# First feed-forward block of a decoder layer: ada products spread over other stages, finished tiles gated in two stages, first channel blocks in written order

## The chip, the core and the metric

One core of a Trainium2 chip runs the whole layer as one program. TensorE (PE; its weight loads are listed as PEld) multiplies, VectorE (DVE), ScalarE (ACT) and GpSimd (POOL) do the elementwise work, and SyncE's queue (SP) issues the DMA transfers in program order. The metric is the time of one execution in microseconds, as the median of the runs.

## What is computed

A decoder layer on x of 256 positions and 1024 channels, float32: a half-step SwiGLU block, a mixer of attention and mLSTM heads, and a second SwiGLU block. Each is preceded by an RMS norm whose scale and shift, and followed by a gate, that come from a vector c.

```python
mod = (c @ w_ada + b_ada).reshape(B, 9, D_MODEL)       # 72 columns of 128 values
sh1, sc1, g1, sh2, sc2, g2, sh3, sc3, g3 = ...
h = modulate(rmsnorm(x, ffn1_norm), sh1, sc1)          # h * (1 + sc) + sh
x = x + 0.5 * (1 + g1) * swiglu(h, w_gate, w_up, w_down)   # D_FF = 2816 = 22 tiles of 128
h = modulate(rmsnorm(x, mix_norm), sh2, sc2)
x = x + (1 + g2) * hybrid_mixer(h, ...)
h = modulate(rmsnorm(x, ffn2_norm), sh3, sc3)
x = x + 0.5 * (1 + g3) * swiglu(h, ...)                # second block, then a final norm
```

## The kernel before

**Products in three passes.** Channels lie on the partitions. Every float32 weight chunk (`raw`, 128 x 2048, 1 MB) is split into a rounded part `whi` (ACT) and the rest `wlo` (DVE), in two pieces of 1024 columns (`split_piece`, lines 199 to 211); activations are split likewise into `hh` and `hl`. `mm3` (line 232) adds whi x hh, wlo x hh and whi x hl. There are 4 buffers for `raw` and 5 each for `whi` and `wlo`. `weights()` (line 219) hands out the next chunk, asks for the load of the chunk three ahead and the split of the next one.

**Ada products.** `ada(col)` (line 247) loads 512 KB of w_ada into one of 3 buffers (one SP transfer) and has DVE multiply it by c and sum it along the row: one column of `mod`. Sixteen columns (scale and shift of the first norm) are made on the spot, two for each of the eight channel blocks. The other 56 are jobs in a list, and `side(...)` (line 551) pops one job for each of its arguments; eight jobs make one of scale, shift or gate.

**First feed-forward block** (`ffn`, k = 0, lines 402 to 494). Each of the 22 tiles of the hidden width needs a gate and an up half, which share one PSUM bank. The work is staged so that the eight channel blocks can be used as they come:
- first blocks: for channel blocks d = 0 to 3, eight tiles (0 to 7) are accumulated in all eight banks. d = 0 is done in plain float32 by `first`, d = 1 to 3 by `outer`, each on one chunk of 48 matmuls. Ahead of block d the program makes the two ada products, the scale, shift and `norm_h` (line 323: DVE `ht`, ACT `hh`, DVE `hl`) and the split of block d + 1. After d = 3 the banks are copied to `half`;
- tiles 8 to 15 on channel blocks 0 to 3 (`inner`, four chunks), then on blocks 4 to 7 (`outer`, four chunks), again in eight banks (`ps`);
- tiles 0 to 7 on channel blocks 4 to 7 (`inner` with d0 = 4, four chunks, lines 481 to 492; below the second inner stage). Each gets a fresh bank, is added to `half`, and is gated by `finish`. Between them the tiles 8 to 15 in `ps` are gated too (`late`), which frees their banks;
- tiles 16 to 21 one by one, then the down projection (11 chunks, 176 pairs of matmuls).

`finish` (line 375) is ACT silu into `sl`, DVE product into `gm`, then ACT and DVE split that into `gh`, `gl`. `sl` and `gm` have two buffers each, given out in program order.

**Banks.** `BANKS` has 2 of tag b, 2 of m and 4 of a. `ring` (line 395) names the tag of each tile of eight: b, m, a, a, b, m, a, a.

**Order.** Instructions sent through `Ordered` with `on` set keep their program order on their engine. All others are put in order by the framework's planner on a simulated timeline when the kernel is built. DMA issues always keep their order. `ordered(d == 0)` (line 451) keeps the written order for the first channel block only.

**After the block.** `residual` (line 358) adds a finished output block to x, and makes that block's part of the next norm's input (`pre_h`) and its square (`add_sq`); `pre_shift` adds the shift's two columns. The first projection of the mixer (`px`, lines 563 to 572) and the mixer follow. Late in the mixer a chain of small steps ends in `rows` (`m_factors`, `spread`), which `m_spread` (PE) needs amid the output projection (`wout`, line 1000).

Of the kernel before, what the change touches and what calls it, by code (L numbers as in the profile page):

```python
# [17 lines left out]
P = 128  # L18
# [42 lines left out]
def layer(ctx: ExitStack, tc: tile.TileContext, i, out: bass.AP):  # L61
# [4 lines left out]
    def ordered(on):  # L66
        for e in (act, dve, pool, pe):
            e.on = on
# [15 lines left out]
    def bank(tag):  # L84
        return psp.tile([P, 512], F32, tag=tag, name=nm("ps" + tag), bufs=BANKS[tag])
# [7 lines left out]
    def const(shape, dt, name):  # L93
        return cst.tile(shape, dt, tag=name, name=name)
# [41 lines left out]
    for k in range(2):  # L136
        pe.matmul(pc[k], ones_r, c_hl[:, k * 512:(k + 1) * 512], start=True, stop=True)
    warm(2)
    act.activation(c_bc[:, 0:512], pc[0], AF.Copy)
    dve.tensor_tensor(sq[:, 0:4], x_sb[:, 0:4], x_sb[:, 0:4], ALU.mult)  # L140
    dve.tensor_tensor(sq[:, 0:2], sq[:, 0:2], sq[:, 2:4], ALU.add)
    act.activation(sq[:, 4:8], x_sb[:, 4:8], AF.Square)
    act.activation(c_bc[:, 512:1024], pc[1], AF.Copy)
    dve.tensor_tensor(sq[:, 4:6], sq[:, 4:6], sq[:, 6:8], ALU.add)

    ident = const([P, P], F32, "ident")
# [19 lines left out]
        pool.affine_select(out=oh32, in_=oh32, compare_op=ALU.not_equal, fill=1.0, base=base,  # L166
                           pattern=[[1, NH], [0, P]], channel_multiplier=-1)
    ohr = const([36, NH, P], F32R, "ohr")
    dve.tensor_copy(ohr, oh32)


    SP = 1024
# [64 lines left out]


    mod = const([P, 72], F32, "mod")
    b1 = const([P, 72], F32, "b1")  # L240
    dve.tensor_scalar(b1, sm[:, 0:72], 1.0, None, ALU.add)
    gs = [const([P, ND], F32, f"gs{k}") for k in range(3)]
    sh = [const([P, ND], F32, f"sh{k}") for k in range(3)]
    gt = [const([P, ND], F32, f"gt{k}") for k in range(3)]
# [36 lines left out]
    def scale_jobs(k):  # L281
        return ada_jobs(24 * k + 8, lambda: scale_fin(k))
# [59 lines left out]
    def hilo(hi, lo, src):  # L342
        act.activation(hi, src, AF.Copy)
        dve.tensor_tensor(lo, src, as32(hi), ALU.subtract)
# [13 lines left out]
    def residual(d, ps, g, k):  # L358
        dve.scalar_tensor_tensor(x_sb[:, d], ps, g[:, d:d + 1], x_sb[:, d], ALU.mult, ALU.add)
        if k is None:  # L360
            s = add_sq(d, pool)
            pool.tensor_scalar(fin_u[0][:, d], x_sb[:, d], sm[:, C_NF + d:C_NF + d + 1], None, ALU.mult)
            return s
        if d == ND - 1:
            s = add_sq(d, pool)
            pre_h(k, d)
        else:
            pre_h(k, d)
            s = add_sq(d, pool)
        return s  # L370
# [4 lines left out]
    def finish(gh, gl, ft, g, u):  # L375
        s = t256("sl")
        act.activation(s, g, AF.Silu)
        m = t256("gm")
        dve.tensor_tensor(m, s, u, ALU.mult)
        hilo(gh[:, ft], gl[:, ft], m)  # L380
# [16 lines left out]
    def ffn(k, nxt):  # L397
        nfa = 3
        with tc.tile_pool(name=f"g{k}", bufs=1) as gp:
            g2 = gp.tile([P, NF, 2, T], F32R, name=f"g2{k}")  # L400
            gh, gl = g2[:, :, 0], g2[:, :, 1]
            if k == 0:
# [45 lines left out]
                parts.append([raws[0][:, k * SP:(k + 1) * SP] for k in range(2)])  # L448
                used[0] += 1
                for d in range(4):  # L450
                    ordered(d == 0)
                    if d < 3:
                        adas(d + 1)
                        load_to(d + 1)
                        fins(d + 1)
                        split_to(d + 1)
                        w = parts[d]
                        used[0] += d > 0
                    else:
                        w = weights()  # L460
                    if d == 0:
                        first(raws[0], ps, h0)
                    else:
                        outer(w, ps, d, False, keep if d == 3 else None)
                    if d == 1:
                        hilo(hh[:, 0, 0:T], hl[:, 0, 0:T], h0)
                ps = [bank(t) for t in ring]
                for j in range(4):
                    w = weights()
# [3 lines left out]
                        inner(w, f2, ps[2 * j + f2], 0, False)  # L473
                for d in range(4, 8):
                    w = weights()
                    if d > 5:
                        side(1, 0)
                    outer(w, ps, d, d == 7)
                late = [lambda ft=ft, pb=pb: finish(gh, gl, 8 + ft, pb[:, 0:T], pb[:, T:2 * T])
                        for ft, pb in enumerate(ps)]  # L480
                for j in range(4):
                    late.pop(0)()
                    late.pop(0)()
                    w = weights()
                    side(1, 1)
                    for f2 in range(2):
                        ft = 2 * j + f2
                        pb = bank(ring[ft])
                        inner(w, f2, pb, 4, True)
                        o = half[:, ft]  # L490
                        dve.tensor_tensor(o, o, pb, ALU.add)
                        finish(gh, gl, ft, o[:, 0:T], o[:, T:2 * T])
                late = []
                nfa = 16
            else:
                ps = [bank(t) for t in ("b", "b", "a", "a", "a", "a")]
# [9 lines left out]
            for ft in range(nfa, NF):  # L506
                if late:
                    late.pop(0)()
                w = weights()
                if late:  # L510
                    late.pop(0)()
                side(*QF[k])
                if k == 0:
                    pb = bank(ring[ft % 8])
                    for d in range(ND):
                        for g in range(2):
                            mm3(pb[:, g * T:(g + 1) * T], w, (d * 2 + g) * P, hh[:, d, 0:T], hl[:, d, 0:T],
                                start=(d == 0 and g == 0), stop=(d == ND - 1))
                    finish(gh, gl, ft, pb[:, 0:T], pb[:, T:2 * T])
                else:  # L520
                    pb = [bank("maba"[ft % 4 - 3]) for g in range(2)]
                    for g in range(2):
                        for d in range(ND):
                            mm3(pb[g][:, 0:W], w, (g * ND + d) * P, hh[:, d], hl[:, d],
                                start=(d == 0), stop=(d == ND - 1))
                    finish_pre(gh, gl, ft, pb[0], pb[1], r)
# [24 lines left out]
    def side(*on):  # L551

        for o in on:
            if jobs:
                jobs.pop(0)(o)


    jobs += scale_jobs(1) + gate_jobs(0) + shift_jobs(1) + gate_jobs(1) + scale_jobs(2) + shift_jobs(2)
    ffn(0, 1)

    px = [bank("a") for _ in range(4)]
    for c in range(2):
        w = weights()
        side(1)
        for d4 in range(4):
            d = c * 4 + d4
            for h in range(NH):
                mm3(px[h][:, 0:W], w, d4 * 512 + h * P, hh[:, d], hl[:, d], start=(d == 0), stop=(d == 7))  # L570
            if d == 0:
                r = rstd_of([acc, nxt_sq[0]], pre=False)
# [15 lines left out]
def mixer(tc, nc, i, mp, L):  # L588
# [377 lines left out]
    m_scores(3)  # L966
    m_sums(1)
    g = tiles(shifted(zs[:, 0]), shifted(zs[:, 1]))
    side(1)
    next(g)  # L970
    next(g0)
    turn(3)
# [26 lines left out]
    po = [bank(t) for t in ("m", "m", "a", "a")]  # L999
    for c in range(4):  # L1000
        w = weights()
        pe.on = c < 2
        for k2 in range(2):
            k = c * 2 + k2
            for d in range(8):
                mm3(po[d // 2][:, (d % 2) * T:(d % 2 + 1) * T], w, (k2 * 8 + d) * P, *mix(k),
                    start=(c == 0 and k2 == 0 and d % 2 == 0), stop=(c == 3 and k2 == 1))
                if (k, d) == (2, 7):
                    m_spread()
                    for h in range(NH):  # L1010
                        m_out(h)
# [90 lines left out]
```

## Time and profile before

| | |
|---|---|
| median of 3 runs | 534.91 us (534.86 to 535.97) |
| the profiled execution | 537.05 us, of which the span from first to last instruction is 535.2 us |
| PE busy | 517.4 us (97%), 3804 matmuls |
| DVE busy | 423.4 us (79%) |
| ACT busy | 281.0 us (53%) |
[...]
| DMA | 125.73 MB, 235 GB/s over the span |

Busy PE time counts a matmul from start to modelled end, and they overlap; how many matmuls start in a stretch says more. A row of the timeline gives start, duration, engine, operation, and in brackets the idle time of that engine just before and what ended it.

### The profile page before, as it was taken

How to read it: one execution, taken by the hardware profiler on the slowest of the kernel's cores; microseconds unless marked ns; L12 is line 12 of the kernel's file. 1: busy time of each engine (PE TensorE's matmuls, PEld its weight loads, DVE VectorE, ACT ScalarE, POOL GpSimd, SP SyncE). 2: the span in 40 equal slices, each digit the busy share in tenths (PEclk: the TensorE clock that was granted, in tenths of full speed). 3: DMA queues.
4: the chain of work that ended last, by engine and by line, in shares of the span. 5: the costliest groups of instructions: out<-in, count | busy, mean ns of one | idle time of the engine just before them, and what ended most of it. 6: DMA issues, size and time to landing. Idle time of an engine off the chain costs nothing.

```text
span 535.2 us, 9560 instructions
## 1 busy us (share of the span) xinstructions
PE 517.4 (97%) x3804; PEld 485.3 (91%) x3804; DVE 423.4 (79%) x714; ACT 281.0 (53%) x486; POOL 46.9 (9%) x64
## 2 busy tenths in 40 slices
PE   7999999899999999999999989999999999999992
PEld 7899999899988889988987889999999999988881
DVE  7898879999889997898885686989986776655423
ACT  4464436355555544566767554865545455544410
POOL 5000000000001110110000020400000000022220
PEclk9999999899999999999999999999999999999998
DMA  8997977988778998578631024488955455455002
GB/s 311 356 411 298 381 282 294 349 351 325 300 286 329 328 344 303 172 287 319 225 146 59 15 105 141 184 326 293 312 195 186 163 196 193 157 206 188 1 1 78
DMA packets 23951, 125.73 MB, mean 235 GB/s; under 512 B 2657, under 2 KB 2913, under 8 KB 14434
## 3 DMA queue, kind: packets, MB, share of 16 engines
q1 hardware_dynamic: 23618, 124.59, 62.2%
q8 instruction: 30, 0.49, 0.4%
q10 hardware_dynamic: 288, 0.52, 0.3%
q14 instruction: 15, 0.12, 0.1%
HBM read 124.05 MB, written 1.05 MB: 234 GB/s over the span
## 4 chain that ended last, share of the span: by engine, by line
PE 89%; DVE 4%; DMA 3%; issue 2%; ACT 1%; SPq 0%; DVEq 0%; ACTq 0%
PE psa L54 42%; PE psb L54 27%; PE psm L54 21%; DMA ada<-in_ada 2%; DMA x<-in_x 1%; DVE junk L54 1%; DVE wlo L54 1%; ACT whi L54 0%; DVE cn L54 0%; DVE u_out L54 0%; ACT sq L54 0%; DVE nw L54 0%; DVE half L54 0%; ACT zs L54 0%; DVE x L54 0%
## 5 line engine op out<-in xcount | busy, mean ns | idle before, releaser
L54 ACT ACTIVATE whi<-raw 128x1024 fp32r<-128x1024 f32 (+1 forms) x160 | 167.2, 1047 | 137.8 <-PE psa L54 62.4
L54 DVE TENSOR_TENSOR wlo<-raw,whi 128x1024 fp32r<-128x1024 f32 (+1 forms) x160 | 193.3, 1211 | 53.2 <-ACT whi L54 51.8
L54 PE MATMUL psa<-hh,whi 128*128 128x258 f32 (+1 forms) x388 | 110.1, 286 | 0.6 <-DVE gm L54 0.6
L54 PE MATMUL psa<-hh,wlo 128*128 128x258 f32 (+1 forms) x388 | 110.3, 286 | 0.0
L54 PE MATMUL psa<-hl,whi 128*128 128x258 f32 (+1 forms) x388 | 108.8, 285 | 0.0
L54 PE MATMUL psb<-hh,whi 128*128 128x258 f32 (+1 forms) x316 | 91.3, 290 | 2.3 <-ACT hh L54 1.2
L54 DVE SCALAR_TENSOR_TENSOR junk<-ada,c_bc 128x1024 bf16<-128x1024 f32 x72 | 88.1, 1224 | 3.4 <-DMA ada<-in_ada 3.3
L54 PE MATMUL psb<-hh,wlo 128*128 128x258 f32 (+1 forms) x316 | 89.4, 284 | 0.0
L54 PE MATMUL psb<-hl,whi 128*128 128x258 f32 (+1 forms) x316 | 88.9, 283 | 0.0
L54 PEld LDWEIGHTS psa<-hh,whi 128*128 128x128 f32 x388 | 74.4, 192 | 0.8 <-DVE gm L54 0.8
L54 PEld LDWEIGHTS psa<-hh,wlo 128*128 128x128 f32 x388 | 74.4, 192 | 0.1
L54 PEld LDWEIGHTS psa<-hl,whi 128*128 128x128 f32 x388 | 73.9, 192 | 0.0
L54 PEld LDWEIGHTS psb<-hh,whi 128*128 128x128 f32 x316 | 59.8, 189 | 5.3 <-issue 1.4
L54 PEld LDWEIGHTS psb<-hh,wlo 128*128 128x128 f32 x316 | 59.7, 189 | 0.1
L54 PEld LDWEIGHTS psb<-hl,whi 128*128 128x128 f32 x316 | 59.7, 190 | 0.0
L54 PE MATMUL psa<-g,whi 128*128 128x512 f32 x176 | 59.4, 395 | 0.0
L54 PE MATMUL psm<-hh,wlo 128*128 128x256 f32 (+1 forms) x200 | 56.9, 285 | 0.0
L54 PE MATMUL psm<-hh,whi 128*128 128x256 f32 (+1 forms) x200 | 56.8, 284 | 0.0
L54 PE MATMUL psm<-hl,whi 128*128 128x256 f32 (+1 forms) x200 | 56.6, 285 | 0.0
L54 PE MATMUL psa<-g,wlo 128*128 128x256 f32 x176 | 45.5, 281 | 0.0
L54 PEld LDWEIGHTS psa<-g,whi 128*128 128x128 f32 x176 | 32.5, 188 | 7.2
L54 PEld LDWEIGHTS psm<-hh,whi 128*128 128x128 f32 x200 | 38.2, 191 | 0.2
(241 smaller groups left out, 768.3 us busy)
## 6 DMA issues: line engine op xcount, KB each, us to landing
ada<-in_ada SPq DMA_DIRECT2D x72, 512.0 KB, 6.0
raw<-in_dn SPq DMA_DIRECT2D x22, 1024.0 KB, 4.8
raw<-in_guB SPq DMA_DIRECT2D x19, 1024.0 KB, 4.8
raw<-in_gu SPq DMA_DIRECT2D x18, 1024.0 KB, 7.1
raw<-in_gu SPq DMA_DIRECT2D x8, 512.0 KB, 7.6
raw<-in_wqk SPq DMA_DIRECT2D x4, 1024.0 KB, 5.8
raw<-in_wout SPq DMA_DIRECT2D x4, 1024.0 KB, 4.8
raw<-in_guA SPq DMA_DIRECT2D x4, 768.0 KB, 4.5
```

Of the source, the lines that this page charges most:

```text
L54: r = f(*a, **k)
```

## The change

Named by its parts:
- **A, start.** Both copies of c to `c_bc` follow each other on ACT. `b1` is made ahead of the last sum of squares. The rounding of `oh32` to `ohr` goes from DVE at the start to ACT in block d = 1.
- **B, first blocks.** The written order is kept for d = 0, 1 and 2.
- **C, ada jobs.** Four in the second outer stage as before, but one for each chunk; in the second inner stage 1 instead of 8; with tiles 16 to 21 5 instead of 6; the down projection keeps 16; `px` takes 4 instead of 2; the late mixer stages `zs` take 3 and 1 instead of none, and the output projection 2. Eight products move from the first block to behind it. The gate of the first block now comes first in the list, the scale of the second norm after it.
- **D, `residual`.** Since that scale comes later, `pre_h` of blocks 0 to 5 is made two at a time with blocks 3, 4 and 5.
- **E, gating.** Of tiles 8 to 15, those in the a banks (2, 3, 6, 7 of `ps`) are gated in the first two chunks of the second inner stage, the other four with tiles 16 and 17. All eight tiles of that stage take a banks; tiles 16 to 21 take a, a, a, a, b, m.

```diff
--- before.py
+++ after.py
@@ -136,11 +136,13 @@
     for k in range(2):
         pe.matmul(pc[k], ones_r, c_hl[:, k * 512:(k + 1) * 512], start=True, stop=True)
     warm(2)
-    act.activation(c_bc[:, 0:512], pc[0], AF.Copy)
+    for k in range(2):
+        act.activation(c_bc[:, k * 512:(k + 1) * 512], pc[k], AF.Copy)
     dve.tensor_tensor(sq[:, 0:4], x_sb[:, 0:4], x_sb[:, 0:4], ALU.mult)
     dve.tensor_tensor(sq[:, 0:2], sq[:, 0:2], sq[:, 2:4], ALU.add)
     act.activation(sq[:, 4:8], x_sb[:, 4:8], AF.Square)
-    act.activation(c_bc[:, 512:1024], pc[1], AF.Copy)
+    b1 = const([P, 72], F32, "b1")
+    dve.tensor_scalar(b1, sm[:, 0:72], 1.0, None, ALU.add)
     dve.tensor_tensor(sq[:, 4:6], sq[:, 4:6], sq[:, 6:8], ALU.add)
 
     ident = const([P, P], F32, "ident")
@@ -166,7 +168,6 @@
         pool.affine_select(out=oh32, in_=oh32, compare_op=ALU.not_equal, fill=1.0, base=base,
                            pattern=[[1, NH], [0, P]], channel_multiplier=-1)
     ohr = const([36, NH, P], F32R, "ohr")
-    dve.tensor_copy(ohr, oh32)
 
 
     SP = 1024
@@ -237,8 +238,6 @@
 
 
     mod = const([P, 72], F32, "mod")
-    b1 = const([P, 72], F32, "b1")
-    dve.tensor_scalar(b1, sm[:, 0:72], 1.0, None, ALU.add)
     gs = [const([P, ND], F32, f"gs{k}") for k in range(3)]
     sh = [const([P, ND], F32, f"sh{k}") for k in range(3)]
     gt = [const([P, ND], F32, f"gt{k}") for k in range(3)]
@@ -361,7 +360,12 @@
             s = add_sq(d, pool)
             pool.tensor_scalar(fin_u[0][:, d], x_sb[:, d], sm[:, C_NF + d:C_NF + d + 1], None, ALU.mult)
             return s
-        if d == ND - 1:
+        if k == 1:
+
+            s = add_sq(d, pool)
+            for j in range(2 * d - 6, 2 * d - 4) if 3 <= d < 6 else range(d, d + 1) if d >= 6 else ():
+                pre_h(k, j)
+        elif d == ND - 1:
             s = add_sq(d, pool)
             pre_h(k, d)
         else:
@@ -448,7 +452,7 @@
                 parts.append([raws[0][:, k * SP:(k + 1) * SP] for k in range(2)])
                 used[0] += 1
                 for d in range(4):
-                    ordered(d == 0)
+                    ordered(d < 3)
                     if d < 3:
                         adas(d + 1)
                         load_to(d + 1)
@@ -464,6 +468,7 @@
                         outer(w, ps, d, False, keep if d == 3 else None)
                     if d == 1:
                         hilo(hh[:, 0, 0:T], hl[:, 0, 0:T], h0)
+                        act.activation(ohr, oh32, AF.Copy)
                 ps = [bank(t) for t in ring]
                 for j in range(4):
                     w = weights()
@@ -473,24 +478,25 @@
                         inner(w, f2, ps[2 * j + f2], 0, False)
                 for d in range(4, 8):
                     w = weights()
-                    if d > 5:
-                        side(1, 0)
+                    side(1)
                     outer(w, ps, d, d == 7)
-                late = [lambda ft=ft, pb=pb: finish(gh, gl, 8 + ft, pb[:, 0:T], pb[:, T:2 * T])
-                        for ft, pb in enumerate(ps)]
+
+                late = [lambda ft=ft: finish(gh, gl, 8 + ft, ps[ft][:, 0:T], ps[ft][:, T:2 * T])
+                        for ft in (2, 3, 6, 7, 0, 1, 4, 5)]
                 for j in range(4):
-                    late.pop(0)()
-                    late.pop(0)()
+                    if j < 2:
+                        late.pop(0)()
+                        late.pop(0)()
                     w = weights()
-                    side(1, 1)
+                    if j == 3:
+                        side(1)
                     for f2 in range(2):
                         ft = 2 * j + f2
-                        pb = bank(ring[ft])
+                        pb = bank("a")
                         inner(w, f2, pb, 4, True)
                         o = half[:, ft]
                         dve.tensor_tensor(o, o, pb, ALU.add)
                         finish(gh, gl, ft, o[:, 0:T], o[:, T:2 * T])
-                late = []
                 nfa = 16
             else:
                 ps = [bank(t) for t in ("b", "b", "a", "a", "a", "a")]
@@ -509,9 +515,10 @@
                 w = weights()
                 if late:
                     late.pop(0)()
-                side(*QF[k])
+                if k or ft > 16:
+                    side(*QF[k])
                 if k == 0:
-                    pb = bank(ring[ft % 8])
+                    pb = bank("aaaabm"[ft - 16])
                     for d in range(ND):
                         for g in range(2):
                             mm3(pb[:, g * T:(g + 1) * T], w, (d * 2 + g) * P, hh[:, d, 0:T], hl[:, d, 0:T],
@@ -555,7 +562,7 @@
                 jobs.pop(0)(o)
 
 
-    jobs += scale_jobs(1) + gate_jobs(0) + shift_jobs(1) + gate_jobs(1) + scale_jobs(2) + shift_jobs(2)
+    jobs += gate_jobs(0) + scale_jobs(1) + shift_jobs(1) + gate_jobs(1) + scale_jobs(2) + shift_jobs(2)
     ffn(0, 1)
 
 
@@ -563,7 +570,7 @@
     px = [bank("a") for _ in range(4)]
     for c in range(2):
         w = weights()
-        side(1)
+        side(1, 0)
         for d4 in range(4):
             d = c * 4 + d4
             for h in range(NH):
@@ -966,7 +973,7 @@
     m_scores(3)
     m_sums(1)
     g = tiles(shifted(zs[:, 0]), shifted(zs[:, 1]))
-    side(1)
+    side(1, 0, 0)
     next(g)
     next(g0)
     turn(3)
@@ -999,6 +1006,7 @@
     po = [bank(t) for t in ("m", "m", "a", "a")]
     for c in range(4):
         w = weights()
+        side(0)
         pe.on = c < 2
         for k2 in range(2):
             k = c * 2 + k2
```

## Rows read from the trace of the kernel before

**Rows 1.** The page: the chain that ended last, by engine.
```profile
PE 89%; DVE 4%; DMA 3%; issue 2%; ACT 1%; SPq 0%; DVEq 0%; ACTq 0%
```

**Rows 2.** By stretch: PE, PEld, DVE, ACT, POOL busy (x instructions), clock, DMA, GB/s.
```profile
20.00:30.00 10.00, 8.82 (x69) 8.49 (x68) 9.04 (x14) 3.69 (x4) 0.00 (x0) 1.00 0.96 355
30.00:40.00 10.00, 10.00 (x86) 10.00 (x85) 8.91 (x14) 6.70 (x9) 0.00 (x0) 1.00 1.01 416
...
90.00:100.00 10.00, 8.27 (x68) 7.87 (x67) 10.00 (x17) 5.40 (x10) 0.00 (x0) 1.00 0.68 263
100.00:110.00 10.00, 10.00 (x74) 10.00 (x73) 10.00 (x21) 3.58 (x6) 0.00 (x0) 0.83 0.98 375
...
160.00:170.00 10.00, 10.00 (x60) 8.79 (x60) 9.97 (x18) 6.96 (x11) 1.90 (x2) 1.00 0.81 308
```

**Rows 3.** Timeline of PE where block d = 1 ends and d = 2 starts.
```profile
26.56 0.29 PE L54 MATMUL psa<-hl,whi 128*128 128x256 f32 x1
28.03 0.39 PE L54 MATMUL psb<-hh,whi 128*128 128x256 f32 x1 [1.18 <-ACT hh L54]
```

**Rows 4.** Timeline of PE in the middle of the second inner stage.
```profile
96.89 0.28 PE L54 MATMUL psm<-hl,whi 128*128 128x256 f32 x1
98.31 0.39 PE L54 MATMUL psb<-hh,whi 128*128 128x256 f32 x1 [1.15 <-ACT whi L54]
99.28 0.39 PE L54 MATMUL psa<-hh,whi 128*128 128x256 f32 x1 [0.58 <-DVE gm L54]
```

**Rows 5.** Timeline of DVE in the second inner stage.
```profile
92.05 0.42 DVE L54 TENSOR_TENSOR gm<-sl,half 128x256 f32<-128x256 f32 x1
...
98.81 0.41 DVE L54 TENSOR_TENSOR gm<-sl,psa 128x256 f32<-128x256 f32 x1
99.15 0.68 DVE L54 TENSOR_TENSOR half<-half,psm 128x512 f32<-128x512 f32 x1
99.74 0.41 DVE L54 TENSOR_TENSOR g<-gm,g 128x256 fp32r<-128x256 f32 x1
```

**Rows 6.** Timeline of ACT in the second inner stage.
```profile
93.48 0.36 ACT L54 ACTIVATE sl<-psa 128x256 f32<-128x256 f32 x1
```

**Rows 7.** Timeline of DVE in the first blocks.
```profile
18.71 1.23 DVE L54 TENSOR_TENSOR wlo<-raw,whi 128x1024 fp32r<-128x1024 f32 x1 [0.46 <-ACT whi L54]
...
20.96 1.23 DVE L54 SCALAR_TENSOR_TENSOR junk<-ada,c_bc 128x1024 bf16<-128x1024 f32 x1 [1.02 <-DMA ada<-in_ada]
22.11 1.22 DVE L54 TENSOR_TENSOR wlo<-raw,whi 128x1024 fp32r<-128x1024 f32 x1
23.24 1.22 DVE L54 SCALAR_TENSOR_TENSOR junk<-ada,c_bc 128x1024 bf16<-128x1024 f32 x1
...
26.95 0.48 DVE L54 SCALAR_TENSOR_TENSOR ht<-x,gs,rr 128x256 f32<-128x256 f32 x1
```

**Rows 8.** Timeline of ACT in the first blocks.
```profile
23.40 1.06 ACT L54 ACTIVATE whi<-raw 128x1024 fp32r<-128x1024 f32 x1 [3.69 <-DMA raw<-in_gu]
...
27.46 0.51 ACT L54 ACTIVATE hh<-ht,sh 128x256 fp32r<-128x256 f32 x1 [1.77 <-DVE ht L54]
28.82 1.06 ACT L54 ACTIVATE whi<-raw 128x1024 fp32r<-128x1024 f32 x1 [0.85 <-DMA raw<-in_gu]
```

**Rows 9.** One SP issue in the first blocks, then its us to landing.
```profile
22.22 0.33 SPq L97 DMA_DIRECT2D ada<-in_ada  x1
...
ada<-in_ada SPq DMA_DIRECT2D x1, 512.0 KB, 4.8
```

**Rows 10.** Timeline of DVE in `px` and late in the mixer.
```profile
214.59 1.23 DVE L54 TENSOR_TENSOR wlo<-raw,whi 128x1024 fp32r<-128x1024 f32 x1 [2.27 <-ACT whi L54]
...
296.32 0.42 DVE L54 SCALAR_TENSOR_TENSOR nw<-rr 128x256 f32<-128x256 f32 x1 [6.36 <-ACT rr L54]
...
311.35 1.95 DVE L54 SCALAR_TENSOR_TENSOR cn<-cn,sm,zs 128x256 f32<-128x256 f32 x2 [1.40 <-ACT zs L54]
```

**Rows 11.** Timeline of PE at the end of the `rows` chain.
```profile
317.30 0.70 PE L54 MATMUL psb<-rows,ohr 36*128 36x256 f32 x4 [1.57 <-DVE rows L54]
```

## The prediction, made before the change was run

> **What bounds the kernel now.** Four views, in this order. The chain that ended last is nine tenths PE [rows 1]: what counts is how long PE stands still or runs at half clock, and what another engine saves is worth only what it saves there. The table by stretch shows where PE loses, by its matmuls, not by its busy share: 86 started between 30 and 40 us, and the second inner stage and the first blocks fall short of that [rows 2]. PE's timeline then gives the gaps and what ended them [rows 3, 4], and the timelines of DVE and ACT around each gap say why the releaser was late [rows 5 to 8].
>
> Loss 1, first blocks. PE's last matmul of block d = 1 starts at 26.56 us, the next at 28.03 [rows 3]: 1.47 us where the spacing is 10 us / 86 = 0.12 [rows 2], so 1.35 us lost. It waits for `hh` of block 2, made by ACT at 27.46 from the `ht` that DVE made at 26.95 [rows 7, 8]. DVE was not late for lack of work: it stood 1.02 us before 20.96, held by the transfer of a product for block 2, and the `wlo` that stood behind it ran only at 22.11 [rows 7].
>
> Loss 2, second inner stage. From 90 to 110 us 68 + 74 matmuls start where 2 x 86 would [rows 2]: 30 missing x 0.116 = 3.5 us. [...] The second wait ends with a `gm` from an a bank at 98.81, whose silu ACT ran at 93.48, just after the `gm` of a tile of `half` at 92.05 [rows 5, 6]: `sl` and `gm` are handed out in program order, so a tile of `ps` in an a bank is gated only after the two tiles of the chunk before, and DVE is full (10.00 of 10 us) [rows 2].
>
> **The sum is made against the profiled execution,** 537.05 us, of which 535.2 us are its span. It lies 2.14 us over the median of 534.91; I take the difference off at the end.
>
> **E and C in the second inner stage.** DVE's prices, start to start: a product 22.11 - 20.96 = 1.15, a `wlo` 23.24 - 22.11 = 1.13 [rows 7], the addition to `half` 99.74 - 99.15 = 0.59, a `gm` 99.15 - 98.81 = 0.34 [rows 5], and as much for the `gl`. Before, four chunks ask DVE for 8 `wlo` (9.0), 8 products (9.2), 16 tiles to gate (16 x 0.68 = 10.9) and 8 additions (4.7): 33.8 us, while PE needs 4 x 48 x 0.12 = 23.0. After: 9.0 + 1 product 1.2 + 12 tiles 8.2 + 4.7 = 23.1 us. DVE goes from 47% too much to just enough, and PE has no reason to wait in the mean.
>
> Does one tile wait? The two first tiles take the banks of `ps` 2 and 3, which are gated first and whose sums end 3.6 and 2.9 us before the outer stage does (five and four eighths of its last chunk's 5.75 us). The third tile needs any free a bank: the first tile's addition to `half` frees one, due 0.59 us after that tile ends, and the next tile's 24 matmuls (2.9 us) run meanwhile. That leaves 2.3 us for what DVE may have in front, two of its largest instructions. Four gatings (2.7 us of DVE) and five products move to or stay with tiles 16 to 21, six chunks of 5.75 us: 12 `wlo` 13.6 + 5 x 1.15 + (6 + 4) x 0.68 = 26 of 34.5 us, so they are covered. I take the whole 3.5 us as gained; the bounds are 0 (it stalls at another bank) and 3.5.
>
> **B, first blocks.** In the written order the second `wlo` of block 1 comes ahead of the product that DVE waits for, in the 1.02 us that DVE stood still: free. Then DVE makes the two products of block 2 (20.96 to 23.3), scale and shift (0.3, an estimate for two instructions of one column) and `ht` (0.4), to 24.0; ACT `hh` (0.5) and, behind it now, the first `whi` (1.0; its data have landed at 23.40 [rows 8]), to 25.6; DVE the first `wlo`, to 26.8. PE is done with block 1 at 26.68 [rows 3]: about 0.2 us of wait instead of 1.35.
>
> Block 3 pays some of it back. Behind the second `wlo` of block 2 (27.9) DVE has `hl` of block 0 (0.4), the two products of block 3 (the later one landed by 22.22 + 4.8 = 27.0 [rows 9], no wait), scale, shift and `ht`, to 31.3; ACT `hh` and `whi` to 32.9; `wlo` at 34.1. Before, that `whi` ran at 28.82 [rows 8], ahead of `hh`. PE is done with block 2 at 26.9 + 5.75 = 32.6. Block 3's matmuls are not in the kept order, so the planner may start with the 16 that need `whi` alone (1.9 us, to 34.8): wait 0.3 us. If it doesn't, PE waits from 32.6 to 34.1, 1.5 us. Net: -1.35 + 0.2 + 0.3 = -0.85 us, taken; bounds -1.35 and +0.35.
>
> [...] The row: a `wlo` stood behind a product that waited for its transfer [rows 7]. [...]
>
> **A.** `ohr` leaves DVE's path to the first norm and `b1` moves into a wait for x: about one `gm`'s 0.34 us by the nearest row [rows 5]. But the first blocks are held by landings afterwards, not by that path [rows 7, 8]. Taken as 0; bounds -0.4 and 0.
>
> **C behind the block.** Eight products come in later: 2 in `px`, 4 in the `zs` stages, 2 in the output projection, each 1.15 us of DVE and one SP transfer with a buffer to wait for; behind it in SP's queue are the weights of three chunks ahead, so a wait there has chunks of 5.75 us to spend. In `px` DVE has a gap of 2.27 us [rows 10], which takes the two. Late in the mixer it stands still 6.36 us before 296.32 [rows 10]: room for five, and the buffers (three) are free by then for at least three of them. The others can fall among the chain that ends in `rows`, for which PE already waits 1.57 us [rows 11]; but that chain has a hole of 1.40 us on DVE too [rows 10]. I take +0.4 us, a third of one product; bounds 0 and +2.3 (the two products of the output projection, whole, on the chain).
>
> **C and D in the down projection.** DVE is full there already (9.97 of 10) [rows 2] and PE doesn't wait. The 16 products stay; the `pre_h` of six blocks comes later but in the same number, two in each of d = 3 to 5, when a block of PE lasts 44 matmuls x 10 us / 60 = 7.3 us [rows 2]. DVE comes in without arrears now. 0; above, one late `wlo`, 1.1 us.
>
> **Sum:** -3.5 - 0.85 + 0 + 0.4 + 0 = -3.95. Profiled execution 533.1 us, median 531.0. All good ends together: 534.91 - 3.5 - 1.35 - 0.4 = 529.7.
>
> **Rivals.**
> - *The written order starves block 3.* For it: every split of block 3 stands behind `hh`, and that behind two products; against it: the planner's freedom in block 3, and a first wait of 1.35 us (at 26.7) after which the clock did not fall (1.00 from 30 to 40 us [rows 2]). Price: B at +0.35 instead of -0.85, and if the clock falls as after loss 2 (3.5 less the waits of 1.3 and 0.85, start to start [rows 4]: 1.4 us), +1.4. Time 534.91 - 3.5 + 0.35 + 1.4 + 0.4 = 533.6. [...]
> - *The second inner stage stalls all the same.* It has only the a banks now and no other to turn to, and DVE at 23.1 of 23.0 us has no slack; a planner that puts products or splits in front of the additions would stop PE as before. Against it: eleven microseconds less to do. Time 534.91 - 0.85 + 0.4 = 534.5: no change that can be measured.
> - *Slower: the moved products lie on the `rows` chain.* Each on it costs 1.15 us of PE's wait one for one. Place: between the norm's steps at 296 and PE's wait at 317. It outweighs the gains of 4.35 us from the fourth product on; with all six of the late stages, 6.9 us, the time is 534.91 - 4.35 + 6.9 = 537.5. Against it: the gap of 6.36 us ahead of the chain.
> - *The late stall goes as well.* The planner lays out the mixer anew; were PE's wait for `rows` gone (1.57 us [rows 11], and 1.4 more if the clock falls behind it as behind loss 2), 528.0.
>
> **How the numbers follow.** The measurement of this kernel can tell about 0.2%, 1.1 us, from no change: faster is below 533.8, slower above 536.0. Chances: forecast 0.57, block 3 starved 0.13 (mostly faster), second inner stage stalls 0.13 (same), slower 0.11, late stall gone 0.06. Faster 0.57 + 0.12 + 0.06 = 0.75, same 0.01 + 0.13 = 0.14, slower 0.11. The range leaves out the slower rival and most of the last: from 529.3, just under all good ends, to 535.2, which takes in the second inner stage stalling with the mixer at a whole product.
>
> **What would show it.** Right: 86 matmuls in every 10 us of the second inner stage and clock 1.00 there; DVE's products gone from it and its full share with them; PE's gap after block 1 at some 0.2 us and a small one after block 2; six products between 285 and 330 us, most of them in DVE's gaps. Wrong: a gap of over 1 us after block 2 (B); a wait of PE for `half` or `gm` near 90 us (E); PE's wait for `rows` grown beyond 1.57 us by multiples of 1.15 (C); a PE wait in the down projection for `wlo` (D).

## The result and the profile after

The changed kernel takes 540.75 us, the kernel before 535.44 (534.86 to 537.16) in the same runs: ratio 1.0088 [1.0065, 1.0111], slower where a gain of 0.7% was forecast. One of its four executions took 1774.33 us (the others 540.03 to 541.15), as one of four of e7 below took 624.82; why is not known, both are left out of the ratios, and without them the medians are 540.36 and 540.79. The trace that came with this result is of the one of 1774.33, so the profile after is that of the same kernel run again (e1 below): 542.33 us, ratio 1.0123 [1.0085, 1.0161], profiled execution 542.23, span 540.4.

First the page of e1: busy time by engine, and the chain that ended last.

```profile
PE 520.2 (96%) x3804; PEld 485.4 (90%) x3804; DVE 424.4 (79%) x713; ACT 283.5 (52%) x488; POOL 50.1 (9%) x64
...
PE 85%; DVE 8%; ACT 2%; issue 2%; DMA 2%; DVEq 0%; ACTq 0%
```

DVE does the same work as before (424.4 us, 423.4 before), but its share of the chain has doubled from the 4% of [rows 1]. Next the table by stretch of e1, with the columns of [rows 2]; the last two stretches are new.

```profile
20.00:30.00 10.00, 9.89 (x79) 9.61 (x78) 8.85 (x15) 3.23 (x5) 0.00 (x0) 1.00 0.99 354
30.00:40.00 10.00, 9.44 (x77) 9.02 (x77) 8.92 (x14) 8.09 (x11) 0.00 (x0) 1.00 0.95 358
90.00:100.00 10.00, 10.00 (x86) 10.00 (x85) 9.40 (x17) 5.38 (x11) 0.00 (x0) 1.00 0.66 236
100.00:110.00 10.00, 10.00 (x86) 10.00 (x85) 9.81 (x17) 7.16 (x14) 0.00 (x0) 1.00 0.60 204
160.00:170.00 10.00, 10.00 (x59) 8.71 (x59) 9.61 (x16) 5.84 (x9) 1.42 (x2) 1.00 0.87 324
280.00:290.00 10.00, 5.11 (x16) 3.56 (x14) 10.00 (x28) 6.76 (x25) 0.00 (x0) 0.60 0.39 144
290.00:300.00 10.00, 10.00 (x62) 6.96 (x60) 1.96 (x7) 5.88 (x16) 0.72 (x1) 0.88 0.00 0
```

The same table of the kernel before has, for those two:

```profile
280.00:290.00 10.00, 10.00 (x68) 8.05 (x68) 8.52 (x24) 8.20 (x25) 0.06 (x1) 1.00 0.19 70
290.00:300.00 10.00, 10.00 (x71) 7.73 (x70) 2.44 (x5) 6.36 (x18) 0.72 (x1) 1.00 0.03 10
```

The second inner stage is mended: 86 + 86 matmuls at clock 1.00 where there were 68 + 74. But between 280 and 290 us PE starts 16 matmuls instead of 68, at a granted clock of 0.60. PE's waits in e1, largest first, and its timeline there:

```profile
PE psm L54 <- DVE wE L54: 4.9, 2, 4.1
PE psb L54 <- DVE rows L54: 1.6, 1, 1.6
```
```profile
279.46 0.74 PE L54 MATMUL psm<-rows,ohr 36*128 36x256 f32 x4
...
284.34 2.95 PE L54 MATMUL psm<-qk,xc 128*128 128x256 f32 x8 [4.15 <-DVE wE L54]
288.04 1.65 PE L54 MATMUL psm<-qk,xc 128*128 128x256 f32 x4 [0.74 <-DVE wE L54]
...
323.36 0.70 PE L54 MATMUL psb<-rows,ohr 36*128 36x256 f32 x4 [1.58 <-DVE rows L54]
```

`wE` are the mLSTM's decay weights. `psm<-qk,xc` are the mLSTM's scores, which `wE` will multiply; they need one of the two m banks, and both hold the spread rows until DVE has read them into `wE`. The weights end a chain of small steps on one engine after another: the gate projections, the gates (`gf`), two running sums (`F`, `nM`), `rows`, its spread over the partitions by PE (279.46), `wE` on DVE. Before, PE never waited for `wE`. The wait for the later `rows` that I watched (at 323.36 in e1) is 1.58 us, as it was [rows 11].

Landmarks divide the difference of the profiled executions (span 540.4 - 535.2 = +5.2 us). Each is the start of a matmul in PE's timeline:

| from ... to | before | e1 | difference |
|---|---|---|---|
| start ... down projection | 146.65 | 142.68 | -3.97 |
| down projection ... `px` | 61.71 | 61.70 | -0.01 |
| `px` ... first product with `mix0h` (output projection) | 98.62 | 108.65 | +10.03 |
| ... last matmul | 218.55 | 217.69 | -0.86 |

The first block gained nearly what the sum has for it (-3.5 - 0.85 = -4.35), and ten microseconds were lost in the mixer: PE's two waits for `wE` make 4.9 of them. The clock makes some 3.6 more, an estimate: in e1's table the granted clock is still 1.00 from 281 to 282 us, 0.53 from 282 to 283 and 0.50 over the whole of 284.34 to 292.34 us, where PE works for all but 0.74 of 8.00 us at half its speed (four score matmuls take 1.65 us at 288.04, and 0.81 in the kernel before, at 281.81 and clock 1.00). (The two rows of 10 us above would give 4.0 + 1.2 = 5.2, but part of that time at the low clock PE stood still anyway.) That leaves 1.5 us that neither explains.

### The profile page after: what moved, and what is told of

It reads as the page before. It is cut to its first block, busy times and chain, and to the rows that moved or that the text cites. A ratio compares the mean times of both kernels' runs of the same rounds, so it can differ in the third digit from the quotient of the medians.

```text
span 1772.5 us, 9569 instructions
## 1 busy us (share of the span) xinstructions
PE 1759.7 (99%) x3804; PEld 1533.1 (86%) x3804; DVE 433.4 (24%) x713; ACT 285.4 (16%) x488; POOL 47.2 (3%) x64
## 4 chain that ended last, share of the span: by engine, by line
PE 99%; DVE 0%; issue 0%; ACT 0%; DVEq 0%; ACTq 0%
PE psa L54 50%; PE psb L54 27%; PE psm L54 22%; DVE u_out L54 0%; DVE wE L54 0%; DVE junk L54 0%; DVE x L54 0%; DVE nw L54 0%; DVEq L1105 0%; ACT rl L54 0%; DVE mx L54 0%; DVE rr L54 0%; ACT rr L54 0%; ACT sq L54 0%; DVE em L54 0%
## 5 line engine op out<-in xcount | busy, mean ns | idle before, releaser
L54 PE MATMUL psa<-hh,wlo 128*128 128x256 f32 (+1 forms) x452 | 312.6, 692 | 0.0
L54 PE MATMUL psa<-hl,whi 128*128 128x256 f32 (+1 forms) x452 | 309.9, 690 | 0.0
L54 PE MATMUL psa<-hh,whi 128*128 128x256 f32 (+1 forms) x452 | 309.1, 685 | 0.0
L54 PEld LDWEIGHTS psa<-hl,whi 128*128 128x128 f32 x452 | 261.4, 581 | 0.4 <-issue 0.4
L54 PEld LDWEIGHTS psa<-hh,whi 128*128 128x128 f32 x452 | 260.7, 578 | 0.2 <-issue 0.2
L54 PEld LDWEIGHTS psa<-hh,wlo 128*128 128x128 f32 x452 | 259.4, 574 | 0.6 <-issue 0.6
L54 PE MATMUL psb<-hh,whi 128*128 128x258 f32 (+1 forms) x284 | 195.8, 690 | 0.0
L54 PE MATMUL psb<-hh,wlo 128*128 128x258 f32 (+1 forms) x284 | 194.0, 683 | 0.0
L54 PE MATMUL psb<-hl,whi 128*128 128x258 f32 (+1 forms) x284 | 193.2, 684 | 0.0
L54 PE MATMUL psa<-g,whi 128*128 128x512 f32 x176 | 185.9, 1092 | 0.0
```

The source lines that it names most:

```text
L54: r = f(*a, **k)
```

## Experiments

All times are medians; ratios are to the kernel before in the same runs, with 95% intervals.

**Which part costs: e1 to e4.** e1 is the changed kernel unaltered; e2 has `ordered(d == 0)` again (without B); e3 has the list of jobs, their places and `residual` of before (without C and D); e4 gates tiles 8 to 15 in the order and the banks of before (without E). All three undo parts of the diff above; of e2 and e4, the lines that matter, against the changed kernel:

```diff
-                    ordered(d < 3)
+                    ordered(d == 0)
```
```diff
-                        for ft in (2, 3, 6, 7, 0, 1, 4, 5)]
+                        for ft, pb in enumerate(ps)]
...
-                        pb = bank("a")
+                        pb = bank(ring[ft])
...
-                    pb = bank("aaaabm"[ft - 16])
+                    pb = bank(ring[ft % 8])
```

> The changed kernel itself once more, for a profile at the usual matmul rate. All theories expect 1.0065 to 1.0111 times the time of before (+3.5 to +6 us). Theory M (the late products lie on the chain that ends in rows): the first block as forecast, 4 us earlier at the start of the down projection than before, and 8 to 10 us lost between 285 and 345 us, in waits of PE for rows or ht behind products. Theory B (the written order starves the first blocks): 4 us or more lost before 45 us. Theory S (the second inner stage stalls for a banks): 4 us or more lost between 80 and 110 us.

> The changed kernel with the written order kept for d = 0 alone, as before. Theory B: 4 us or more come back, about 536 us or less. Theories M and S: no gain, 540 us, or a little more if the written order was worth the 0.85 us of the forecast.

> The changed kernel with the ada jobs and residual as before, so parts A, B and E alone. Theory M: the late mixer is as before, at most 536 us; with DVE full again in the second inner stage some of the loss there may come back. Theory S: slower than the changed kernel, as DVE is 47 per cent over in a stage with a banks alone, 543 us or more. Theory B: 540 us.

> The changed kernel with gating and banks of the second inner stage as before, so A, B, C and D. Theory S: 4 us or more come back, 536 us or less. Theory M: no gain, 540 us or some more, as tiles of ps in a banks are gated late again. Theory B: 540 us.

Measured: e1 542.33; e2 543.58, 1.0140 [1.0098, 1.0182]; e3 533.46, 0.9956 [0.9941, 0.9971]; e4 543.26, 1.0137 [1.0103, 1.0172]. Only taking C and D away helps, by 8.9 us. (The start of e2 holds a wait of PE for `c_bc` of 2.2 us that e1 hasn't; the intervals of the two overlap.) In e4 PE waits 4.9 us for `wE` just as in e1; in e3 not at all. Yet e4's down projection starts at 143.33, 3.3 earlier than before, and its second inner stage has all its matmuls, so the moved products free that stage without E as well. The table by stretch of e4:

```profile
90.00:100.00 10.00, 10.00 (x86) 10.00 (x86) 9.18 (x16) 5.45 (x11) 0.00 (x0) 1.00 0.64 229
100.00:110.00 10.00, 10.00 (x86) 10.00 (x85) 9.27 (x16) 7.08 (x16) 0.00 (x0) 1.00 0.55 214
```

**E alone: e8.** The kernel before with the gating order and the banks of the change, nothing else (the diff of part E).

> The kernel before with part E alone: gating order and banks of the second inner stage. If the stall there (3.5 us) came from the order of the banks: 531 to 532.5 us, with 86 matmuls in every 10 us of that stage though DVE is asked for 47 per cent more than it has. If it came from DVE's load, as the forecast's sum has it: 534 us or more, with waits for half or gm.

Measured: 532.59, 0.9936 [0.9916, 0.9957], faster than the kernel before and the changed one; only e9 and e15 below, at 532.60 and 532.74, are as fast. The down projection starts at 142.99, 3.66 us earlier than before. The table by stretch of e8:

```profile
90.00:100.00 10.00, 10.00 (x86) 10.00 (x85) 10.00 (x18) 5.78 (x11) 0.00 (x0) 1.00 0.69 263
100.00:110.00 10.00, 10.00 (x86) 10.00 (x86) 10.00 (x17) 5.21 (x8) 0.00 (x0) 1.00 0.79 295
```

All eight products are still there and DVE is full, 10.00 of 10, as in [rows 2]; yet PE starts 86 in each. The order of gating and the choice of banks, which e8 changes together, free the banks in time; no product had to move. (E also takes four gatings out of the stage: by the prediction's prices DVE is still asked for 33.8 - 2.7 = 31.1 us in 23.0.)

**Taking the late products' work away: e5, e6, e11.** The last six (e5) or three (e6) of the 48 jobs lose DVE's sum along the row, a copied value stands in their columns of `mod`, and their transfers stay; in e11 the six have neither sum nor transfer, only a copied value. From e5's edit against the changed kernel:

```diff
         dma(t, i["ada"][col])
+        if lite[0]:
+            dve.tensor_copy(mod[:, col:col + 1], t[:, 0:1])
+            return
```

> The changed kernel, with the multiply-and-sum of the last six of the 48 jobs (columns 2 to 7 of the third shift) left out: the 512 KB transfers stay, and DVE only copies one column in place of the 1.15 us. So those six values of mod are wrong. Theory G (the planner puts the six late products among the gate chain gf, F, na, nM, rows, wE, and PE waits for wE): the wait for wE is gone, 531 to 534 us. Theory T (their transfers hold up the weights behind them in the queue of SP): 540 us or more. Theory P (the loss comes from residual's later pre_h, or from the two added products in px): 539 us or more.

> The same with the last three of the six alone left out (columns 5 to 7). Theory G: PE's wait for wE shrinks by about as much as the left-out ones among the chain take, from 4.9 to 2 us or so, and the clock falls less; 535 to 538 us. Theories T and P: 540 us or more.

> The changed kernel without DVE's sums and without the transfers of the last six jobs (six columns of mod get a copied value, so these columns are not computed). Theory 'transfers of the late six': about 533.5 (537.65 with the transfers). Theories 'extra products in px' and 'list order and D': no change from 537.65.

Measured: e5 537.65, 1.0033 [1.0018, 1.0048]; e6 539.80, 1.0073 [1.0056, 1.0090]; e11 540.06, 1.0079 [1.0052, 1.0107]. Without the sums the kernel gains 2.5 us for three, 4.7 for six. Nothing points to the transfers: without them the kernel is slower than e5, not faster. Why the same six, left out in two ways, differ by 2.4 us is taken up below.

**Other places for the six: e7.** Three behind the last `wE`, two and one in chunks 2 and 3 of the output projection, kept in the written order on DVE:

```diff
-    side(1)
...
-        side(0)
+        dve.on = True
+        side(*[0] * (0, 0, 2, 1)[c])
+        dve.on = False
```

> All work kept, but the six late products are held on DVE in written order: three directly behind the last product of wE, where DVE stood still 6.36 us before, two and one behind m_out in the last two chunks of the output projection. Theory G: 531 to 534 us with all 48 products made, so that it is their place and not their number. Theories T and P: 539 us or more. A loss at the rows chain or at the start of the second feed-forward block, 1.15 us for each product that lies on it, would mean that there is no free place for six.

Measured: 540.79 (540.44 to 543.13), 1.0103 [1.0071, 1.0135]: no clear gain over e1, whose interval it overlaps. PE's waits for `wE` shrink to 3.7 us only, and its wait for `hh` in the output projection grows from 0.3 us to 1.5.

**The places alone, and the two in `px`: e9, e10.** e9 is the changed kernel, with its list (gate first), A, B, D and E, but every product at the place of before; e10 has then two more in `px` and two fewer in the second inner stage. The first diff is e9 against the changed kernel, the second e10 against e9.

```diff
-                    side(1)
+                    if d > 5:
+                        side(1, 0)
                     outer(w, ps, d, d == 7)
...
-                    if j == 3:
-                        side(1)
+                    side(1, 1)
...
-                if k or ft > 16:
-                    side(*QF[k])
+                side(*QF[k])
...
-        side(1, 0)
+        side(1)
         for d4 in range(4):
...
-    side(1, 0, 0)
...
-    side(1)
...
-        side(0)
```
```diff
-                    side(1, 1)
+                    side(*(1, 1)[:1 + (j < 2)])
...
-        side(1)
+        side(1, 0)
         for d4 in range(4):
```

> The changed kernel with its list of jobs (gate of the first block first), D, A, B and E, but the products popped at the places of before: 4 in the second outer stage, 8 in the second inner stage, 6 with tiles 16 to 21, 16 in the down projection, 2 in px, 12 in the mixer, none later. All the work is done. Open: 4.2 us by which the kernel without the sums of the last six (537.65) is still slower than the one with jobs and residual as before (533.46). Theory 'two extra products in px delay the start of the gate chain': about 533.5. Theory 'the late six's transfers in SP's queue do it': about 533.5. Theory 'the new order of the list and the deferred pre_h (D) do it': about 537.5.

> As the run before, but two products more in px (4, as in the changed kernel) and two less in the second inner stage (6). All the work is done. Theory 'extra products in px': about 537.5, with the gates' function gf at some 254 us instead of 248. Theory 'transfers of the late six': about 533.5. Theory 'list order and D': about 537.5, the same as the run before.

Measured: e9 532.60, 0.9944 [0.9921, 0.9967]; e10 535.14, 0.9996 [0.9979, 1.0012]. So A, B, D and the order of the list together cost nothing; the places cost 9.7 us: 2.5 for the two in `px`, 7.2 for the rest. The two were to fill a DVE gap of 2.27 us [rows 10]. DVE's timeline of e10 in `px`:

```profile
208.16 0.08 DVE L54 DVE_READ_ACCUMULATOR junk<-ada,c_bc 128x1 f32 x1
210.50 1.23 DVE L54 TENSOR_TENSOR wlo<-raw,whi 128x1024 fp32r<-128x1024 f32 x1 [2.27 <-ACT whi L54]
...
211.98 1.22 DVE L54 SCALAR_TENSOR_TENSOR junk<-ada,c_bc 128x1024 bf16<-128x1024 f32 x1
```

The gap is still there, 2.27 us: the products run ahead of it and after it, none in it, in front of other work.

**Is it an order on ACT? e12, e13.** In e10, as in e1, the fourth convolution's SiLU (`xc`) stands on ACT behind the first head's exponentials, and the gates start 5 us later than in e9. e12 (on e10) and e13 (on e1) keep the written order of these two on ACT.

```diff
+        act.on = h == 3
         act.activation(xc[:, h], cv, AF.Silu)
+        act.on = False
...
+        act.on = j == 0
         for e in range(2):
...
+        act.on = False
         dve.reciprocal(ri, su)
```

> As the run with 4 products in px and the other places of before (535.14), but ACT keeps the written order between the fourth xc (SiLU) and the first head's four exponentials. Theory 'the order on ACT costs the 2.5 us': xc at some 244 us instead of 248.9, gf at some 249 to 250 instead of 253.6, time 532.6 to 533.2. Rival 'the DVE time of the two products costs it, 1.15 us each': 535.1, unchanged.

> The changed kernel with the same order kept on ACT (xc of the fourth convolution before the first head's exponentials); all the work is done. Theory 'order on ACT for the px products, DVE time for the six late ones': 542.3 - 2.5 = 539.8. Rival 'all eight cost their DVE time, wherever the gates begin': 542.3, unchanged.

Measured: e12 535.27, 0.9997 [0.9983, 1.0011], against e10's 535.14; e13 541.35, 1.0108 [1.0085, 1.0132], against e1's 542.33. The theory falls. ACT's timeline of e10, then of e12:

```profile
248.90 0.42 ACT L54 ACTIVATE xc<-gm 128x256 f32<-128x256 f32 x1
```
```profile
244.81 0.42 ACT L54 ACTIVATE xc<-gm 128x256 f32<-128x256 f32 x1
```

`xc` came 4.1 us earlier, as wanted, and the first `wE` not: 278.74 us in e12, 277.55 in e10.

**How many products stand before `wE`: e14, e15.** e14 is the changed kernel with `px` at two (and three in the second inner stage); e15 is e9 with two products more in the second outer stage, so that the mixer has ten instead of twelve.

```diff
-                    if j == 3:
+                    if j:
                         side(1)
...
-        side(1, 0)
+        side(1)
         for d4 in range(4):
```
```diff
-                    if d > 5:
-                        side(1, 0)
+                    side(*(1, 1)[:1 + (d > 5)])
                     outer(w, ps, d, d == 7)
```

> The changed kernel with px at 2 products as before and 3 instead of 1 in the second inner stage; the six late products stay late. Theory 'two costs that add': 542.3 - 2.5 = 539.8, that is 532.6 + 6 x 1.2 for the late six. Rival 'the late six cost only when the gates begin late': near 534.

> The places of before with the changed list (532.6), but the second outer stage pops 6 products instead of 4, so that the mixer has 10 instead of 12. Theory 'a product in the mixer costs its DVE time in either direction': 532.6 - 2 x 1.15 = 530.3. Rival 'below the number of before DVE no longer sets the chain' (PE's wait for rows of the norm chain and the gates' own products does): 532.6. Against both: if the second outer stage has no room on DVE or in the transfers (DVE 73 to 90% busy there, the DMA share 0.7 to 1.0), PE waits there and it is 533 to 535.

Measured: e14 538.92, 1.0065 [1.0038, 1.0091]; e15 532.74, 0.9951 [0.9932, 0.9971]. Five kernels that all do the whole work now differ in little but the number of products between the first block and the first `wE`. DVE's groups, from its last `x` of the first block to that `wE`, give the number; these are the lines of the products in e15, e9, e10, e14 and e1:

```profile
L54 DVE SCALAR_TENSOR_TENSOR junk<-ada,c_bc 128x1024 bf16<-128x1024 f32 x12 | 14.6, 1221 | 0.0
```
```profile
L54 DVE SCALAR_TENSOR_TENSOR junk<-ada,c_bc 128x1024 bf16<-128x1024 f32 x14 | 17.0, 1216 | 0.1
```
```profile
L54 DVE SCALAR_TENSOR_TENSOR junk<-ada,c_bc 128x1024 bf16<-128x1024 f32 x16 | 19.4, 1213 | 0.0
```
```profile
L54 DVE SCALAR_TENSOR_TENSOR junk<-ada,c_bc 128x1024 bf16<-128x1024 f32 x18 | 21.8, 1212 | 0.1
```
```profile
L54 DVE SCALAR_TENSOR_TENSOR junk<-ada,c_bc 128x1024 bf16<-128x1024 f32 x20 | 24.3, 1213 | 0.3 <-DVE ri L54 0.3
```

| kernel | products | DVE, block's end to first `wE` | PE waits for `wE` | PE, `px` to `mix0h` | median |
|---|---|---|---|---|---|
| e15 | 12 | 65.8 us | 0 | 99.2 | 532.74 |
| e9 | 14 | 68.4 | 0 | 98.7 | 532.60 |
| e10 | 16 | 72.5 | 0.2 | 101.3 | 535.14 |
| e14 | 18 | 74.5 | 2.8 | 105.4 | 538.92 |
| e1 | 20 | 77.7 | 4.9 | 108.7 | 542.33 |

The kernel before has 14, 68.4 and 98.6. From 12 to 20 each product more moves `wE` by (77.7 - 65.8) / 8 = 1.5 us: its own 1.2, and some more because later splits come in front too (the same view counts 16 `wlo` in e9 and 18 in e1). DVE stands idle for 9.4 us of this stretch with 14 products and for 7.7 with 20 (the brackets of its timeline summed): the gaps come from waits for ACT and PE, and a product seldom falls into one. From 12 to 14 products PE's part doesn't grow, which is why e15 gains nothing; above, it does.

PE's timeline shows how much room there was. In e1 the first score matmul starts 1.42 us after `wE` does (284.34 - 282.92); in e9 it starts 4.28 us after (278.37, `wE` at 274.09), with PE busy on other matmuls until then:

```profile
278.37 0.81 PE L54 MATMUL psm<-qk,xc 128*128 128x256 f32 x4
```

So in e9 `wE` could come 2.9 us later before PE would wait for it; in the kernel before it is 2.8 (281.81, `wE` at 277.55). At 1.5 us each that is two products, and the waits in the table go that way: 0.2 us with two more than in e9, 2.8 with four, 4.9 with six. (The time of the two is another matter: e10 takes 2.5 us more almost without that wait; see what stays open.)

DVE's timeline shows it at one step. In e9 `wE` follows the spread (PE, 273.57) at once, and DVE had stood idle for it:

```profile
274.09 2.69 DVE L54 SCALAR_TENSOR_TENSOR wE<-psm,nac,maskt 128x256 f32<-128x256 f32 x8 [2.57 <-PE psm L54]
```

In e1 the spread ends at 279.46 + 0.74 = 280.20, and `wE` starts 2.7 us later:

```profile
276.42 1.21 DVE L54 SCALAR_TENSOR_TENSOR junk<-ada,c_bc 128x1024 bf16<-128x1024 f32 x1
...
278.53 0.41 DVE L54 TENSOR_TENSOR rows<-nM,rows 4x256 fp32r<-4x256 f32 x1
...
280.44 1.22 DVE L54 SCALAR_TENSOR_TENSOR junk<-ada,c_bc 128x1024 bf16<-128x1024 f32 x1
...
281.58 1.23 DVE L54 TENSOR_TENSOR wlo<-raw,whi 128x1024 fp32r<-128x1024 f32 x1
282.71 0.27 DVE L54 TENSOR_SCALAR em<-em 4x256 f32<-4x256 f32 x1
282.92 2.67 DVE L54 SCALAR_TENSOR_TENSOR wE<-psm,nac,maskt 128x256 f32<-128x256 f32 x8
...
295.20 0.55 DVE L54 TENSOR_TENSOR wE<-wE,psm 128x384 f32<-128x384 f32 x1 [3.80 <-PE psm L54]
```

A product ahead of `rows` and a product and a split ahead of `wE`: none of them is needed by either. They stand there because the planner is free in the order of the products, and put them there. The hole late in the mixer that was to take them is there too (3.80 us at 295.20, from 6.36 at 296.32 in [rows 10]), after the harm.

**What stays open.** The number of products doesn't settle the time alone. e5, e7 and e11 have 16 before `wE` like e10, but 73.7 to 74.7 us to it instead of 72.5, and PE waits 2.8 to 3.7 us for `wE`, much as in e14 with its 74.5 us; e5 and e11 have less work than e10 and take 2.5 and 4.9 us more. Their instructions come in another order on every engine. On PE it shows: between the spread and the first scores stand 30 other matmuls in e9 and in the kernel before, 15 and 16 in e10 and e12, 6 in e5, e7 and e11, none in e14 and e1. With 15 or more there PE hardly waits for `wE`, with 6 or none it does. Why the planner leaves so few there isn't known; e12 and e13 show that the order of `xc` isn't the reason. e11 and e5 differ on top of that in the clock: behind the wait for the later `rows` it is 0.83 from 320 to 330 us in e11 and 1.00 in e5, which is 0.9 us after the last landmark (218.59 us against 217.71); another 0.9 is in the waits for `wE` (3.7 us against 2.8).

So the sizes for single products (1.2 us each from e9 to e1, 9.7 / 8, of which six stand before the first `wE`) hold to within such shifts. Nor are PE's named waits the whole cost: in e10 they (0.2 us for `wE`, 0.6 for `pT`) make only 0.8 of the 2.6 us between `px` and `mix0h`, and in e12, with 73.3 us to `wE`, PE doesn't wait for it at all and takes the same 2.6 us more.

## Why the prediction was wrong, point by point

- **E and C, second inner stage, -3.5 us: right in size, half of it not needed.** E alone brings -3.66 (e8). I argued that DVE had 47% too much to do and that eight products less made it fit. In e8 and e9 none moves away, and PE doesn't stall; in e8 DVE is full (10.00 of 10 us, with 86 matmuls started): with the tiles in a banks gated early, a full DVE is no bound there, since its other work can also run later. In e4 it is the other way round, the old order and lighter DVE, and PE doesn't stall either. As far as e4 and e8 show, the stall needed both, and taking away one was enough. Whether in E the order of gating or the banks did it was not run.
- **B, first blocks, -0.85 us: too much.** The wait after block 1 fell from 1.35 us to 0.26, as forecast (0.2). The one after block 2 was put at 0.3. PE's timeline of e1 has two there, both for a `whi`, the later one for the second piece of the split, which I had left out of the step:

```profile
33.07 0.39 PE L54 MATMUL psb<-hh,whi 128*128 128x256 f32 x1 [0.36 <-ACT whi L54]
...
34.02 0.39 PE L54 MATMUL psb<-hh,whi 128*128 128x256 f32 x1 [0.20 <-ACT whi L54]
```

  Start to start they cost 0.53 and 0.37 us. In all 1.2 us of waits instead of 1.35, and from 20 to 40 us 79 + 77 = 156 matmuls where there were 155 [rows 2]. That is the first rival's mechanism without its fall of the clock (1.00). A, B, D and the order of the list together bring nothing that can be measured: 532.60 with them (e9), 532.59 without (e8).
- **A and D, 0: right, as far as is shown.** The down projection takes 61.70 us in e1, 61.71 before. A was run only together with B and D.
- **C behind the block, +0.4, bounds 0 and +2.3: the step that failed.** It was +10.0 us in the profiled executions, 9.7 in the medians (e9 to e1). It read two gaps on DVE as room, 2.27 us in `px` and 6.36 us late in the mixer [rows 10], and bounded the cost by the two products of the output projection. The gaps were real, but the products didn't go there: the first stayed at 2.27 us (e10), and of the six that were meant for later only two ran behind the start of `wE`. And the chain to which they were added is not the one that I had watched: not the second `rows` at 317, whose wait stayed at 1.57 to 1.58 us, but the gates' chain to `wE` at 277, 40 us earlier, where the kernel before showed no wait at all. It showed no wait because PE came to the scores 2.8 us later than `wE` would have allowed, room for two products at most, and six more came to stand before it. The views that would have told are PE's timeline at its first scores, and DVE's busy time ahead of `wE`, 59 of 68.4 us (68.4 less 9.4 idle).
- **The slower rival** had the mechanism, each product on a chain at its own price, and said 537.5 with six. Place and number were wrong: eight products cost (two of them those of `px`), the chain is an earlier one, and the clock falls with the wait (0.60 from 280 to 290 us in e1).
- **Standing behind other work.** The first rival had it against B; it bore on C: in e1 `wE` could have started by 280.20 and stood behind a product and a split until 282.92.

## What to carry to other kernels

Before work is moved to another stage, look for what the other engines take from this one there, and measure how much later it could come before they wait: here that was 2.8 us, and beyond it the other engine stood still. Even what fits in need not be free: two products more cost 2.5 us (e10), and the waits explain only a part. Gaps that are waits for someone else don't count as room: the 2.27 us in `px` stayed with two products more (e10). Work that waits for nothing but its transfer runs where the planner likes, so look for it in the trace, not at its line. And an engine at 100% need not be the bound: freeing the banks in another order brought the whole gain by itself, and no version is faster than the kernel before with that part alone (0.9936).

## What was unexpected of the hardware

PE's wait for the later `rows` is nearly the same in all kernels (1.50 to 1.59 us), but what the clock does after it is not. The table by stretch of the kernel before, around its wait of 1.57 us at 317.30 [rows 11], then of e9, around one of 1.58 us at 313.90:

```profile
310.00:320.00 10.00, 8.43 (x65) 8.12 (x63) 8.59 (x13) 5.20 (x7) 3.22 (x4) 0.93 0.23 81
320.00:330.00 10.00, 10.00 (x78) 10.00 (x78) 6.11 (x13) 4.09 (x7) 0.00 (x0) 0.90 0.41 137
```
```profile
310.00:320.00 10.00, 8.13 (x65) 7.61 (x64) 9.90 (x17) 4.43 (x8) 1.59 (x2) 1.00 0.39 131
320.00:330.00 10.00, 10.00 (x86) 10.00 (x85) 5.83 (x13) 4.66 (x10) 0.40 (x1) 1.00 0.35 132
```

The granted clock falls to 0.93 and 0.90 in the one (taken by single microseconds it is 0.50 from 319 to 321 us and 1.00 again from 322 on), and stays at 1.00 in the other; the next stretch has 8 matmuls fewer, 0.9 us, which is the last landmark's difference. The length of this wait didn't decide it. All the traces but the one of 1774.33 us fall in two groups by this: from `mix0h` to the last matmul the nine without a fall here take 217.6 to 217.7 us (e1, e2, e4, e5, e8, e9, e13 to e15), the seven with one 218.5 or more (the kernel before, e3, e6, e7, e10 to e12). So e3's 0.9 us over e8 (533.46 and 532.59) need not come from its parts A and B. Executions of the kernel before in the runs of e1 lie between 533.83 us (mean clock 0.995) and 537.39 (0.986), so part of its spread may be this.
